# Hybrid decoder layer on one core: score blocks of gated linear attention collected in a compact tile

## The chip, the cores and the metric

The kernel runs on one core of one Trainium2 chip. The metric is device time in microseconds (us) of one execution. A core has five engines with instruction streams of their own: TensorE (PE in the profile; its weight loads are listed as PEld), VectorE (DVE), ScalarE (ACT), GpSimd (POOL) and SyncE (SP), which here issues the DMAs. They wait for each other through semaphores.

## The reference

One decoder layer over 2048 frames with 16 meta tokens in front, all float32. A norm and one combined projection feed three mixers: attention with forget gates (FoX, 8 heads), gated linear attention (GLA, 4 heads, 64 keys, 128 values each) and a gated linear recurrence (LRU, width 1024). Their gated outputs go through one output projection, a norm and the residual sum.

```
proj = rms_norm(h, pre_g) @ w_in
fq, fk, fv, ff, fg, gq, gk, gv, ga, gg, lx, lg = split(proj)
y_fox = fox_attention(fq, fk, fv, log_sigmoid(ff + b_f)) * silu(fg)
log_a = log_sigmoid(ga @ w_a2 + b_a) / 16
o     = gla(gq, gk, gv, log_a)        # S_t = diag(a_t) S_(t-1) + k_t^T v_t;  o_t = q_t S_t
y_gla = o * rsqrt(mean(o*o) + eps) * gla_norm_g * silu(gg)
y_lru = rg_lru(conv(lx), w_r, b_r, w_i, b_i, lam) * silu(lg)
out   = h + rms_norm(concat(y_fox, y_gla, y_lru) @ w_out, post_g)
```

The change is in the GLA part. Inside 128 positions the kernel computes a masked score block: element (s, t), for s <= t, is the sum over the 64 keys of k_s q_t exp(b_t - b_s), with b the running sum of log_a.

## The kernel before

**Stages.** Projections (`proj_cm`, L465; `proj_tm`, L477) are 24 matmuls each: 8 slices of the model width, and fp16 high and low halves in three products. The mixers run one after the other: GLA first (100 to 545 us in the profile), then LRU, FoX, and the output projection. The program is a list of jobs (`jobs`, L194 to 217). A job has weight loads, a `prep` generator that issues the projections for it, a `mix` generator with the mixer's own arithmetic, and two numbers. `merge` (L155) steps the mix of one job and the prep of the next in turn: over the first `n_main` steps of the mix it spreads `n_fill` steps of the prep, and what is left of either is issued at the end. A step is what stands between two `yield`s; a projection is one to three of them. GLA has eight such mixes: two pairs of heads (hp 0 and 1), each over four chunks of 512 positions; with them stand the projections of the next chunk, beside the last one those of the first LRU job. LRU has 40 jobs (8 width tiles, 5 pieces each). Within an engine instructions run in the order of issue, which a scheduler has settled when the program is built.

**A GLA chunk (`gla_mix`).** The two heads of a pair hold 64 partitions each, and a chunk is four blocks i of 128 positions. A block's 128x128 scores are built by levels. The two widest (64 and 32) are plain rectangles off the diagonal. The diagonal 32x32 blocks take level 0 (the plain product, of which only the diagonal counts) and five levels 16, 8, 4, 2, 1, each right for another part of the block. For a level, GpSimd subtracts (L956, L957), ScalarE takes the exponential (L958) and VectorE multiplies with keys and queries (L959, L960) into a tile `lv`; TensorE then computes sixteen 32x32 blocks a head, 32 matmuls (`L992`, 64x32 weights and 32 columns, float32) into PSUM, with one bank for each head (tag `st`, two banks). VectorE copies each into `at`, a [128, 4, 128] tile of SBUF for each head, where a mask of bytes says so: `copy_predicated` L999, four partition groups of 32 by two heads, so 8 instructions a level of 32 partitions x 4 x 32 elements. The next level's scores take the same two banks, so they wait for those copies. For level 0 VectorE multiplies by the identity instead (L1009, 8 instructions), TensorE also computes the wide rectangles (L1005), and ScalarE copies these into `at` (L1014). GpSimd has set `at` to zero before (L978).

At the chunk's end 16 matmuls with `at` (L1023) and 16 with the carried state S (L1027), float32, add up to the chunk's output in two banks (`pv`). This closing run is issued without a `yield` in it. What follows (L1033 to L1048) squares, gates and norms it.

**Other names.** `gate` is the output gate (tanh on ScalarE L501, product on VectorE L502), `gv` the evacuated value projection (ScalarE L754), `mx` banks for small sums. `norm_apply` (L389 to L393) normalizes the next 512 columns of the input and splits them in fp16 halves; it runs inside the prep of the first chunks. `fa_mix` (L645) multiplies the 16-row gate projection by w_a2 (L659), in a bank of tag `st`, which ScalarE evacuates (L660); its log-sigmoid ends in L679. PSUM has eight banks: `pj` (projections), `mx`, `st` and `pv`, two each.

Of the kernel before, what the change touches and what calls it, by code (L numbers as in the profile page):

```python
# [40 lines left out]
LEVELS = (64, 32, 16, 8, 4, 2, 1)  # L41
# [38 lines left out]
GAP = 2  # L80
# [7 lines left out]
class Ctx:  # L88
# [6 lines left out]


BUFS = {"A0": 3, "A2": 3, "KA": 6, "KB": 6, "QA": 2, "QB": 2, "B0": 2, "B1": 2, "B2": 2, "B3": 2, "V": 6, "G": 2, "R": 1,
        "T": 3, "ZZ": 4, "WC": 1, "OO": 3, "OX": 2, "LV": 5, "AT": 4, "GV": 6, "GG": 6, "GS": 6, "M": 1, "MV": 1, "YG": 2, "RS": 2, "ZS": 1, "ZA": 2, "PT": 6, "ED": 2, "KT": 1, "Z": 1, "WH": 1, "WL": 1, "XC": 4, "X": 16, "L0": 4, "L1": 4, "L2": 2, "L3": 2, "L4": 6}


def unit(k, tag, shape, dt=F32, name=None):
    wide = tag in ("QA", "QB", "KA", "KB", "WC", "OO", "OX", "T", "Z", "ZZ", "WH", "WL")
# [64 lines left out]
def hybrid_kernel(tc, xT, x, w_grp, w_fa, vecs, w_a2, w_r, w_i, w_out, post_g, masks, out, yD=None):  # L167
    nc = tc.nc
    with ExitStack() as es:
        k = Ctx()  # L170
# [20 lines left out]
        norm_scale(k)  # L191
        start = beside(first_project(k), gla_first(k, FIRST_FA, 0), FA0)

        jobs = [([], start, chain(gla_meta(k, 0), gla_mix(k, 0, 0)), 11 + GAP, 0)]  # L194
        for c in range(1, NCH):
            f = [(NM + CH * c + CH // 2 * i, CH // 2) for i in range(2)]
            load = {2: [("gk", 1), ("gv", 1, 0), ("gv", 1, 1), ("gq", 1), ("gg", 1, 0), ("gg", 1, 1)]}
            jobs.append((load.get(c, []), chain(fa_project(k, f), beside(gla_project(k, 0, c), gla_first(k, f, c), FA1)),
                         gla_mix(k, 0, c), 8 + GAP, 28))
        sums = forget_sums(k)  # L200
        for c in range(NCH):
            load = {2: [("lx", 0), ("lg", 0)]}
# [737 lines left out]
def gla_mix(k, hp, c):  # L940
# [35 lines left out]
    for h in range(2):  # L976
        with k.tc.issue_after(pool):
            nc.gpsimd.memset(at[h], 0.0)  # L978
    steps = (0,) + LEVELS[2:]
    for li, C in enumerate(steps):  # L980
# [14 lines left out]
        for h in range(2):
            hs = slice(64 * h, 64 * h + 64)
            if C:
                for s in parts:
                    nc.vector.copy_predicated(at[h][s, :, s], k.masks[s, li - 1:li, s].to_broadcast([32, 4, 32]),  # L999
                                              sps[h][s, :, s])  # L1000
                continue
            for W, xw in wide:
                for i in range(4):
                    for s0 in range(0, P, 2 * W):
                        nc.tensor.matmul(out=sps[h][s0:s0 + W, i, s0 + W:s0 + 2 * W],  # L1005
                                         lhsT=xw[hs, i * P + s0:i * P + s0 + W],
                                         rhs=xw[hs, i * P + s0 + W:i * P + s0 + 2 * W], start=True, stop=True)
            for s in parts:
                nc.vector.tensor_tensor(at[h][s, :, s], sps[h][s, :, s],  # L1009
                                        k.ident[s, s].unsqueeze(1).to_broadcast([32, 4, 32]), op=ALU.mult)  # L1010
# [623 lines left out]
```

## Time and profile before

| | us |
|---|---|
| timed runs | 2058.44, 2058.95, 2049.12 (median 2058.44) |
| the profiled execution's own time | 2055.92 |
| its span, first to last recorded instruction | 2054.2 |
| TensorE busy | 1930.0 (94%) |
| VectorE busy | 1324.5 (64%) |
| ScalarE busy | 995.9 (48%) |
| GpSimd busy | 584.0 (28%) |
| GLA stage | 100 to 545 |

The profile records one execution. Busy time of an engine is the sum of its instructions; a matmul's end is modelled. "Idle before" is the time an engine stood still in front of a group of instructions, with the engine and the line that ended it. The granted clock is the share of TensorE's full clock (2.4 GHz) that it was given in a stretch; 0.50 is 1.2 GHz.

### The profile page before, as it was taken

To read this page: it belongs to the slowest core of one execution; us is meant where nothing else is said; L and a number is where in the kernel's file an instruction comes from. 1 tells how busy PE (TensorE), PEld (TensorE's weight loads), DVE (VectorE), ACT (ScalarE), POOL (GpSimd) and SP (SyncE) were. 2 spreads that over 40 slices of the span, in tenths; PEclk is the share of its full clock that TensorE was granted. 3 is DMA by queue.
4 is the path that set the end of the run, shared out by engine and by line. 5 is a ranking of instruction groups with operands and counts; after the bars stand their busy time and mean duration, and the time that the engine had idled before them with its cause. 6 is when DMAs were issued, how large, how long until landed. Compare 5 with 4: busy or idle time off the path is not lost. (4 is left out here: it accounts for less than half of the span.)

```text
span 2054.2 us, 39995 instructions
## 1 busy us (share of the span) xinstructions
PE 1930.0 (94%) x16240; PEld 1024.9 (50%) x16240; DVE 1324.5 (64%) x3038; ACT 995.9 (48%) x1489; POOL 584.0 (28%) x571
## 2 busy tenths in 40 slices
PE   7888989999999999999999999999999968989998
PEld 5555666556555556556434443444344323634443
DVE  6777464666687778784576357435734565887664
ACT  7744632335588888872334233422332356544441
POOL 3334122223333333331112111211121113443532
PEclk9899889899899999999999999999999989999999
DMA  6200120111211111110022002100200132734321
GB/s 221 68 9 28 40 83 29 34 51 33 90 46 42 42 42 46 42 63 7 13 56 67 13 12 56 49 13 22 73 2 22 32 112 74 251 114 131 122 91 62
DMA packets 92266, 123.37 MB, mean 60 GB/s; under 512 B 16936, under 2 KB 59624, under 8 KB 92080
## 3 DMA queue, kind: packets, MB, share of 16 engines
q1 hardware_dynamic: 92080, 120.81, 18.7%
q8 instruction: 127, 2.08, 0.4%
q14 instruction: 59, 0.48, 0.1%
HBM read 94.03 MB, written 26.65 MB: 59 GB/s over the span
## 5 line engine op out<-in xcount | busy, mean ns | idle before, releaser
L465 PE MATMUL pj<-xhl,whl 128*128 128x512 f16 (+3 forms) x3960 | 807.0, 356 | 19.4 <-DVE at L999 7.1
L465 PEld LDWEIGHTS <-whl 128*128 128x128 f16 x3984 | 365.8, 98 | 394.5 <-issue 59.9
L1243 ACT ACTIVATE pt<-sq,consts 128x1024 f32<-128x1024 f32 (+4 forms) x176 | 163.0, 926 | 281.2 <-PE sq L1241 152.3
L1185 DVE CUSTOM_DVE_ANT_0 mj<-mq,CB 128x512 bf16<-128x512 f32 (+4 forms) x344 | 189.7, 580 | 85.5 <-PE mq L1181 47.0
L1251 POOL TENSOR_TENSOR za<-za,pt 128x512 f32<-128x512 f32 (+1 forms) x80 | 98.2, 1227 | 397.4 <-ACT pt L1243 361.7
L477 PEld LDWEIGHTS <-xhl 128*128 128x128 f16 (+1 forms) x3264 | 191.1, 99 | 39.4 <-issue 34.6
L1251 DVE TENSOR_TENSOR za<-za,pt 128x512 f32<-128x512 f32 (+3 forms) x208 | 124.9, 627 | 118.0 <-ACT pt L1243 117.8
L477 PE MATMUL pj<-whl,xhl 128*128 128x128 f16 (+1 forms) x3024 | 196.0, 223 | 3.3 <-ACT gv L754 3.3
L1259 PE MATMUL fv<-pt,fv 128*64 128x512 f32 (+4 forms) x704 | 170.3, 531 | 0.4 <-ACT pt L1243 0.4
L1564 PEld LDWEIGHTS <-whl 128*128 128x128 f16 x1008 | 98.8, 98 | 126.3 <-issue 10.3
L1235 PE MATMUL sq<-QA,KA 64*128 64x512 f16 (+4 forms) x1032 | 128.5, 342 | 13.5 <-ACT pt L1243 13.1
L1564 PE MATMUL pj<-ts,whl 128*128 128x512 f16 x576 | 129.8, 385 | 6.0 <-ACT ts L1337 4.6
L999 DVE COPY_PREDICATED at<-consts,st 32x128 f32<-32x128 uint8 x320 | 94.6, 296 | 19.6 <-PE st L992 10.7
L543 DVE SCALAR_TENSOR_TENSOR xc<-lx,consts,xc 128x448 f32<-128x448 f32 (+1 forms) x120 | 94.8, 790 | 3.5
L1564 PE MATMUL pj<-xhl,whl 128*128 128x512 f16 x432 | 95.4, 379 | 0.0
L1544 PE MATMUL pj<-xhl,yhl 128*128 128x256 f16 (+1 forms) x576 | 89.2, 312 | 0.3 <-DVE xhl L1338 0.3
L1278 POOL TENSOR_TENSOR fo<-fo,rz 128x512 f32<-128x512 f32 x16 | 21.3, 1334 | 221.3 <-DMA rz<-rowD 165.9
L1235 PEld LDWEIGHTS <-KA 64*128 64x128 f16 (+1 forms) x1032 | 42.1, 94 | 79.8 <-issue 59.9
L1526 POOL TENSOR_TENSOR o<-o,xt 128x512 f32<-128x512 f32 x31 | 50.8, 1657 | 99.3 <-DVE o L1523 48.9
L958 ACT ACTIVATE lv<-lv 128x512 f32<-128x512 f32 x56 | 34.9, 626 | 91.0 <-POOL lv L957 90.9
L501 ACT ACTIVATE gate<-pj,consts 128x512 f32<-128x512 f32 (+2 forms) x72 | 46.1, 640 | 67.6 <-PE pj L465 67.1
L1235 PE MATMUL sq<-QA,KX 64*128 64x512 bf16 (+4 forms) x344 | 68.3, 341 | 8.8 <-DMA QA<-dr 8.8
(260 smaller groups left out, 2920.4 us busy)
## 6 DMA issues: line engine op xcount, KB each, us to landing
raw<-in_w_grp_dram SPq DMA_DIRECT2D x44, 512.0 KB
raw<-in_w_out_dram SPq DMA_DIRECT2D x32, 512.0 KB
y<-yD SPq DMA_DIRECT2D x32, 512.0 KB
CB<-c32D SPq DMA_DIRECT2D x32, 256.0 KB
xt<-in_x_dram SPq DMA_DIRECT2D x16, 512.0 KB
out_dram<-o SPq DMA_DIRECT2D x32, 256.0 KB
yD<-yl SPq DMA_DIRECT2D x32, 224.0 KB
xr<-in_xT_dram SPq DMA_DIRECT2D x24, 256.0 KB
```

Of the source, the lines that this page charges most:

```text
L465: nc.tensor.matmul(out=ps, lhsT=a[:, kt, 0:m], rhs=b[:, kt, u0:u0 + n], start=i == 0, stop=i == 23)
L477: nc.tensor.matmul(out=ps, lhsT=a[:, kt, u0:u0 + m], rhs=b[:, kt, :], start=i == 0, stop=i == 23)
L543: nc.vector.scalar_tensor_tensor(out=xc, in0=lx[:, j:j + n], scalar=cw(j), in1=xc, op0=ALU.mult, op1=ALU.add)
L999: nc.vector.copy_predicated(at[h][s, :, s], k.masks[s, li - 1:li, s].to_broadcast([32, 4, 32]), sps[h][s, :, s])
L1185: nc.vector.tensor_tensor_reduce(out=junk[:, h, 0:n], in0=ps[:, h, 0:n], in1=d.cb[pc][:, h, 0:n], scale=1.0, scalar=-3e38, op0=ALU.add, op ...
L1235: nc.tensor.matmul(out=sp[0:m, h, off:], lhsT=a[j // 4][hs, kk], rhs=b[hs, off:], start=i == 0, stop=i == 3 and d < 0)
L1243: nc.scalar.activation(pt[0:m, :, off:], sp[0:m, :, off:], AF.Exp, scale=K.esc[0:m])
L1251: eng.tensor_tensor(out=za[h][0:m, off:], in0=za[h][0:m, off:], in1=pt[0:m, h, off:], op=ALU.add)
L1259: nc.tensor.matmul(out=pv[hs, off1:], lhsT=V1[0:m1, j1 % 4, hs], rhs=pt1[0:m1, h, off1:], start=j1 == 0, stop=j1 == nj - 1)
L1526: eng.tensor_tensor(out=o, in0=o, in1=xt[:, h, :], op=ALU.add)
L1544: nc.tensor.matmul(out=po, lhsT=a, rhs=cut(w, r), start=i == 0, stop=i == 3 * OT - 1)
L1564: nc.tensor.matmul(out=ps, lhsT=a[:, kt, :], rhs=b(kt), start=kt + j == 0, stop=(kt, j) == (KT - 1, 2))
```

## The change

**Score blocks.** The two tiles `at` become one [128, 8, 128]. The diagonal blocks are gathered in a new compact tile `ac` [128, 8, 32]: partition group s of 32 rows holds its own 32 columns. Masks and identity are laid out in the same way at the start of the program (`load_consts`). All 32x32 blocks of a level go to the same 128 columns of a bank, so that one `copy_predicated` for each head takes all 128 partitions: 2 instead of 8 a level. PSUM: the two `st` banks become one pair `gs`. Level 0 has a pair for itself, and the five levels share a second allocation of it, four levels side by side in slots of 128 columns (the fifth takes the first slot again). At the chunk's end eight copies, four on VectorE and four on ScalarE, bring `ac` into `at`, and a `yield` follows. The closing run gets a `yield` after two of its four blocks.

**Steps.** n_main goes from 8 + GAP to 10 + GAP (11 to 13 in the first chunk of a pair of heads), n_fill from 28, 34 and 24 to 23, 25 and 20, the number of steps that the prep has. The first two LRU jobs become one job, whose prep stands beside the last GLA mix. LRU jobs without a store take n_main 3 in place of 4.

**Bank of the gate projection.** `fa_mix` takes its bank from `pj` in place of `st`.

```
-BUFS: "AT": 4                      +BUFS: "AT": 2 (wide), "AC": 2
 def hybrid_kernel
-   ... gla_mix(k, 0, c), 8 + GAP, 28))
+   ... gla_mix(k, 0, c), 10 + GAP, 23))
-   ... gla_mix(k, 1, c), 8 + GAP, 24))
+   ... gla_mix(k, 1, c), 10 + GAP, 20))
-   jobs.append((load.get((t, c), []), lru_project(k, t, c), lru_mix(k, t, c, ...), 4, 6))
+   if (t, c) == (0, 1):
+       w, prep0, mix0, n0, n_fill = jobs.pop()
+       jobs.append((w, chain(prep0, prep), chain(mix0, mix), n0 + 4, n_fill + 6))
+   else:
+       jobs.append((load.get((t, c), []), prep, mix, 4 if flush else 3, 6))
 def load_consts
-   nc.gpsimd.tensor_copy(k.masks, mf[:, 2:, :])
+   for s0 in range(0, P, 32):
+       s = slice(s0, s0 + 32)
+       nc.gpsimd.tensor_copy(k.masks[s], mf[s, 2:, s])
+       nc.vector.tensor_copy(k.identc[s], k.ident[s, s])
 def fa_mix
-   pz = bank(k, "st")
+   pz = bank(k)
 def gla_mix
-   at = [unit(k, "AT", [P, 4, P], name="at") for _ in range(2)]
+   at = unit(k, "AT", [P, 8, P], name="at").rearrange("p (h i) t -> p h i t", h=2)
+   ac = unit(k, "AC", [P, 8, 32], name="ac").rearrange("p (h i) t -> p h i t", h=2)
    for li, C in enumerate(steps):
-       sps = [blocks(bank(k, "st")) for _ in range(2)]
+       if li < 2:
+           sp = pair(k, "gs")
+           if C: sv = sp.rearrange("p h (l i t) -> p l h i t", l=4, t=32)
+           else: sb = sp.rearrange("p h (i t) -> p h i t", t=P)
+       sc = sv[:, (li - 1) % 4] if C else sb[:, :, :, 0:32]
-       matmul(out=sps[h][s, i, s], lhsT=xk[hs, e], rhs=xq[hs, e])
+       matmul(out=sc[s, h, i], lhsT=xk[hs, e], rhs=xq[hs, e])
-       for s in parts: copy_predicated(at[h][s, :, s], k.masks[s, li - 1:li, s], sps[h][s, :, s])
+       copy_predicated(ac[:, h], k.masks[:, li - 1:li, :], sc[:, h])
-       for s in parts: tensor_tensor(at[h][s, :, s], sps[h][s, :, s], k.ident[s, s], op=mult)
+       tensor_tensor(ac[:, h], sc[:, h], k.identc, op=mult)
        yield
+   for j, s in enumerate(parts):
+       for h in range(2):
+           (nc.vector.tensor_copy if j < 2 else nc.scalar.copy)(out=at[s, h, :, s], in_=ac[s, h])
+   yield
    for i in range(4):
        matmul(os[h][:, s], lhsT=V[h][:, i, :], rhs=at..., start=True, stop=False)
        matmul(os[h][:, s], lhsT=S[hs, i, :], rhs=qd[hs, s], start=False, stop=True)
+       if i == 1: yield
```

Lines move by 11 in the helpers and by up to 22 in `gla_mix`: L465 becomes L476, L477 L488, L660 L671, L999 L1012, L1009 L1024, L1014 L1029, L1023 L1043, L1027 L1047; the copies out of `ac` are L1034.

The order of instructions on an engine, before and after, at three places. First VectorE at the end of the fifth chunk (first chunk of the second pair of heads), before; L959 and L960 are level products, L502 a gate, L1035 the chunk's output:

```order
L999 COPY_PREDICATED at<-consts,st 32x4x32 x8
L959 TENSOR_TENSOR lv<-lv,ks 128x16x16
L960 TENSOR_TENSOR lv<-lv,qs 128x16x16
L999 COPY_PREDICATED at<-consts,st 32x4x32 x8
L959 TENSOR_TENSOR lv<-lv,ks 128x32x8
L960 TENSOR_TENSOR lv<-lv,qs 128x32x8
L502 SCALAR_TENSOR_TENSOR gate<-gate,pj 128x512
L999 COPY_PREDICATED at<-consts,st 32x4x32 x8
L959 TENSOR_TENSOR lv<-lv,ks 128x64x4
L960 TENSOR_TENSOR lv<-lv,qs 128x64x4
```

and after, where L970 and L971 are the level products, L1012 the masked copies and L513 the gate:

```order
L1012 COPY_PREDICATED ac<-consts,gs 128x128 x2
L971 TENSOR_TENSOR lv<-lv,qs 128x8x32
L971 TENSOR_TENSOR lv<-lv,qs 128x16x16
L970 TENSOR_TENSOR lv<-lv,ks 128x32x8
L971 TENSOR_TENSOR lv<-lv,qs 128x32x8
L1012 COPY_PREDICATED ac<-consts,gs 128x128 x2
L1034 COPY at<-ac 32x4x32 x4
L970 TENSOR_TENSOR lv<-lv,ks 128x64x4
L971 TENSOR_TENSOR lv<-lv,qs 128x64x4
L513 SCALAR_TENSOR_TENSOR gate<-gate,pj 128x512
L1057 SCALAR_TENSOR_TENSOR yg<-pv,consts,gate 128x512 x2
```

The gate, which stood between the level products and the last copies, now comes behind the copies out of `ac`.

Second TensorE at the same place, before: the last projection, and the start of the closing run (the run goes on as it begins, with 16 of each line):

```order
L465 LDWEIGHTS whl
L465 MATMUL pj<-xhl,whl 128x512
L1023 MATMUL pv<-at,gv 128x128
L1027 MATMUL pv<-qd,S 128x128
L1023 MATMUL pv<-at,gv 128x128
L1027 MATMUL pv<-qd,S 128x128
L1023 MATMUL pv<-at,gv 128x128 x2
L1027 MATMUL pv<-qd,S 128x128
L1023 MATMUL pv<-at,gv 128x128
L1027 MATMUL pv<-qd,S 128x128
L1023 MATMUL pv<-at,gv 128x128
L1027 MATMUL pv<-qd,S 128x128 x2
```

and after:

```order
L476 LDWEIGHTS whl
L476 MATMUL pj<-xhl,whl 128x512
L1043 MATMUL pv<-at,gv 128x128 x2
L1047 MATMUL pv<-qd,S 128x128 x2
L1043 MATMUL pv<-at,gv 128x128 x2
L1047 MATMUL pv<-qd,S 128x128 x2
L476 LDWEIGHTS whl
L476 MATMUL pj<-xhl,whl 128x512
L476 LDWEIGHTS whl
L476 MATMUL pj<-xhl,whl 128x512
```

The run is cut behind the second block; 8 projections follow, and then the other half. In front of the first half stand 24 projections where 8 stood before.

Third VectorE in the second chunk, where the norm of the next input columns is applied (L389, L393; after L400, L404), before:

```order
L389 SCALAR_TENSOR_TENSOR xr<-xr,consts,mx 128x512
L393 TENSOR_TENSOR xhl<-xr,xhl 128x512
L389 SCALAR_TENSOR_TENSOR xr<-xr,consts,mx 128x512 x3
L393 TENSOR_TENSOR xhl<-xr,xhl 128x512
L389 SCALAR_TENSOR_TENSOR xr<-xr,consts,mx 128x512
L393 TENSOR_TENSOR xhl<-xr,xhl 128x512
L1009 TENSOR_TENSOR at<-st,consts 32x4x32 x8
L959 TENSOR_TENSOR lv<-lv,ks 128x128x2
L960 TENSOR_TENSOR lv<-lv,qs 128x128x2
L959 TENSOR_TENSOR lv<-lv,ks 128x256
L960 TENSOR_TENSOR lv<-lv,qs 128x256
L999 COPY_PREDICATED at<-consts,st 32x4x32 x13
```

and after:

```order
L400 SCALAR_TENSOR_TENSOR xr<-xr,consts,mx 128x512 x3
L404 TENSOR_TENSOR xhl<-xr,xhl 128x512
L400 SCALAR_TENSOR_TENSOR xr<-xr,consts,mx 128x512
L404 TENSOR_TENSOR xhl<-xr,xhl 128x512
L400 SCALAR_TENSOR_TENSOR xr<-xr,consts,mx 128x512 x3
L404 TENSOR_TENSOR xhl<-xr,xhl 128x512
L400 SCALAR_TENSOR_TENSOR xr<-xr,consts,mx 128x512
L690 SCALAR_TENSOR_TENSOR z<-z,e 128x1024
L404 TENSOR_TENSOR xhl<-xr,xhl 128x512
L1012 COPY_PREDICATED ac<-consts,gs 128x128 x2
L852 SCALAR_TENSOR_TENSOR b<-consts,z 128x128 x4
L970 TENSOR_TENSOR lv<-lv,ks 128x256
```

The norm stood ahead of level 0 (L1009) before and stands now between the masked copies of two levels (rows ahead of it: L1012 x2). L690, the last step of the log-sigmoid (L679 before), stands inside it.

## Rows read from the trace of the kernel before

**Rows 1.** The page: span, and TensorE's busy time with the other engines'.
```profile
span 2054.2 us, 39995 instructions
PE 1930.0 (94%) x16240; PEld 1024.9 (50%) x16240; DVE 1324.5 (64%) x3038; ACT 995.9 (48%) x1489; POOL 584.0 (28%) x571
```

**Rows 2.** Stretches: us, busy us of engines (instructions), clock, DMA share, GB/s.
```profile
100.00:545.00 445.00, 408.84 (x6157) 265.14 (x6157) 278.21 (x759) 175.99 (x298) 125.42 (x164) 0.90 0.13 39
545.00:1290.00 745.00, 731.36 (x4832) 380.33 (x4830) 511.52 (x1155) 436.27 (x599) 206.40 (x235) 1.00 0.14 44
```

**Rows 3.** Groups, 100 to 545 us: busy us, mean ns | idle before, who ended it.
```profile
L465 PE MATMUL pj<-xhl,whl 128*128 128x512 f16 x648 | 157.1, 395 | 9.1 <-DVE at L999 7.1 <-ACT at L1014 2.0
L999 DVE COPY_PREDICATED at<-consts,st 32x128 f32<-32x128 uint8 x320 | 94.6, 296 | 19.6 <-PE st L992 10.7
...
L1023 PE MATMUL pv<-at,gv 128*128 128x128 f32 x128 | 34.9, 387 | 8.3 <-DVE at L999 8.2
...
L992 PE MATMUL st<-lv 64*32 64x32 f32 x2560 | 33.2, 204 | 9.8 <-DVE at L999 8.9 <-DVE lv L960 0.9
...
L960 DVE TENSOR_TENSOR lv<-lv,qs 128x256 f32<-128x256 f32 x51 | 30.5, 605 | 0.2
...
L959 DVE TENSOR_TENSOR lv<-lv,ks 128x256 f32<-128x256 f32 x51 | 26.1, 512 | 16.5 <-ACT lv L958 15.5
...
L1009 DVE TENSOR_TENSOR at<-st,consts 32x128 f32<-32x128 f32 x64 | 18.3, 287 | 12.8 <-PE st L1005 11.2
...
L389 DVE SCALAR_TENSOR_TENSOR xr<-xr,consts,mx 128x512 f32<-128x512 f32 x16 | 11.2, 738 | 3.2 <-PE mx L380 3.2
...
L393 DVE TENSOR_TENSOR xhl<-xr,xhl 128x512 f16<-128x512 f32 x8 | 7.6, 947 | 3.4 <-ACT xhl L391 3.4
...
L659 PE MATMUL st<-ga,wa 16*128 16x256 f32 x16 | 6.6, 578 | 2.2 <-ACT at L1014 1.3 <-PE pj L477 0.9
...
L477 PE MATMUL pj<-whl,xhl 128*16 128x128 f16 x48 | 5.5, 295 | 3.3 <-ACT gv L754 3.3
...
L679 DVE SCALAR_TENSOR_TENSOR z<-z,e 128x1024 f32<-128x1024 f32 x3 | 4.6, 1535 | 0.2 <-ACT e L678 0.2
...
L465 PE MATMUL pj<-xhl,whl 128*128 128x16 f16 x24 | 0.8, 171 | 1.9 <-DVE gate L502 1.9
```

**Rows 4.** Timeline, fifth chunk's end: start, us, instruction, count [idle before, releaser].
```profile
381.47 0.76 PE L992 MATMUL st<-lv 64*32 64x32 f32 x64
...
382.16 1.90 PE L465 MATMUL pj<-xhl,whl 128*128 128x512 f16 x8
...
382.31 0.42 DVE L959 TENSOR_TENSOR lv<-lv,ks 128x256 f32<-128x256 f32 x1
...
382.66 0.83 DVE L960 TENSOR_TENSOR lv<-lv,qs 128x256 f32<-128x256 f32 x1
...
383.52 0.69 DVE L502 SCALAR_TENSOR_TENSOR gate<-gate,pj 128x512 f32<-128x512 f32 x1
...
384.12 2.58 DVE L999 COPY_PREDICATED at<-consts,st 32x128 f32<-32x128 uint8 x8
...
385.54 0.46 PE L1023 MATMUL pv<-at,gv 128*128 128x128 f32 x2 [1.48 <-DVE at L999]
```

**Rows 5.** Stretches, as rows 2: five of the eight closing runs.
```profile
205.60:214.80 9.20, 9.20 (x34) 6.61 (x36) 1.91 (x6) 0.00 (x0) 0.00 (x0) 0.53 0.00 0
274.40:283.90 9.50, 9.50 (x33) 6.80 (x34) 2.14 (x10) 0.00 (x0) 0.00 (x0) 0.50 0.23 82
332.20:337.70 5.50, 5.46 (x33) 4.04 (x34) 1.87 (x6) 0.00 (x0) 0.00 (x0) 1.00 0.00 0
385.50:393.90 8.40, 8.36 (x32) 6.04 (x32) 1.87 (x6) 0.00 (x0) 0.00 (x0) 0.59 0.00 0
523.80:533.30 9.50, 9.50 (x32) 6.83 (x32) 5.12 (x10) 1.05 (x1) 0.00 (x0) 0.50 0.03 9
```

**Rows 6.** Timeline, as rows 4: a run of short projections.
```profile
306.89 2.85 PE L477 MATMUL pj<-whl,xhl 128*128 128x128 f16 x48
```

More of the change, by code (lines that the diff above doesn't have):

```diff
@@ L97 @@
 BUFS = {"A0": 3, "A2": 3, "KA": 6, "KB": 6, "QA": 2, "QB": 2, "B0": 2, "B1": 2, "B2": 2, "B3": 2, "V": 6, "G": 2, "R": 1,
-        "T": 3, "ZZ": 4, "WC": 1, "OO": 3, "OX": 2, "LV": 5, "AT": 4, "GV": 6, "GG": 6, "GS": 6, "M": 1, "MV": 1, "YG": 2, "RS": 2, "ZS": 1, "ZA": 2, "PT": 6, "ED": 2, "KT": 1, "Z": 1, "WH": 1, "WL": 1, "XC": 4, "X": 16, "L0": 4, "L1": 4, "L2": 2, "L3": 2, "L4": 6}
+        "T": 3, "ZZ": 4, "WC": 1, "OO": 3, "OX": 2, "LV": 5, "AT": 2, "AC": 2, "GV": 6, "GG": 6, "GS": 6, "M": 1, "MV": 1, "YG": 2, "RS": 2, "ZS": 1, "ZA": 2, "PT": 6, "ED": 2, "KT": 1, "Z": 1, "WH": 1, "WL": 1, "XC": 4, "X": 16, "L0": 4, "L1": 4, "L2": 2, "L3": 2, "L4": 6}
 def unit(k, tag, shape, dt=F32, name=None):
-    wide = tag in ("QA", "QB", "KA", "KB", "WC", "OO", "OX", "T", "Z", "ZZ", "WH", "WL")
+    wide = tag in ("AT", "QA", "QB", "KA", "KB", "WC", "OO", "OX", "T", "Z", "ZZ", "WH", "WL")
     n = 1
@@ L192, in hybrid_kernel @@
         start = beside(first_project(k), gla_first(k, FIRST_FA, 0), FA0)
-        jobs = [([], start, chain(gla_meta(k, 0), gla_mix(k, 0, 0)), 11 + GAP, 0)]
+        jobs = [([], start, chain(gla_meta(k, 0), gla_mix(k, 0, 0)), 13 + GAP, 0)]
         for c in range(1, NCH):
@@ L204, in hybrid_kernel @@
                 jobs.append(([], chain(gla_project(k, 1, -1), gla_project(k, 1, 0)),
-                             chain(gla_meta(k, 1), gla_mix(k, 1, 0)), 11 + GAP, 34))
+                             chain(gla_meta(k, 1), gla_mix(k, 1, 0)), 13 + GAP, 25))
             else:
-                jobs.append((load.get(c, []), gla_project(k, 1, c), gla_mix(k, 1, c), 8 + GAP, 24))
+                jobs.append((load.get(c, []), gla_project(k, 1, c), gla_mix(k, 1, c), 10 + GAP, 20))
         lru0 = len(jobs)
@@ L215, in hybrid_kernel @@
                     load = {(7, 0): [("fk", 0), ("fv", 0)], (7, 2): [("fq", 0), ("fg", 0)]}
-                jobs.append((load.get((t, c), []), lru_project(k, t, c),
-                             lru_mix(k, t, c, (5 * t + c) % 2 == 1), 4, 6))
+                flush = (5 * t + c) % 2 == 1
+                prep, mix = lru_project(k, t, c), lru_mix(k, t, c, flush)
+                if (t, c) == (0, 1):
[3 more added lines that the diff above has]
+                    jobs.append((load.get((t, c), []), prep, mix, 4 if flush else 3, 6))
         for p in range(4):
@@ L291, in load_consts @@
     nc = k.nc
-    k.masks = carve(k, (len(LEVELS) - 2) * P // 4).bitcast(U8).rearrange("p (l t) -> p l t", t=P)
+    k.masks = carve(k, (len(LEVELS) - 2) * 8).bitcast(U8).rearrange("p (l t) -> p l t", t=32)
+    k.identc = carve(k, 32)
     mf = unit(k, "T", [P, len(LEVELS), P], name="mf")
     nc.sync.dma_start(out=mf, in_=k.ins["masks"])
-    nc.gpsimd.tensor_copy(k.masks, mf[:, 2:, :])
+    for s0 in range(0, P, 32):
+        s = slice(s0, s0 + 32)
+        nc.gpsimd.tensor_copy(k.masks[s], mf[s, 2:, s])
+        nc.vector.tensor_copy(k.identc[s], k.ident[s, s])
 def pow2_scale(k, sq, scale, inv, mul=None):
@@ L973, in gla_mix @@
     k.st["S"] = nS
-    at = [unit(k, "AT", [P, 4, P], name="at") for _ in range(2)]
-    for h in range(2):
-        with k.tc.issue_after(pool):
-            nc.gpsimd.memset(at[h], 0.0)
+    at = unit(k, "AT", [P, 8, P], name="at").rearrange("p (h i) t -> p h i t", h=2)
+    ac = unit(k, "AC", [P, 8, 32], name="ac").rearrange("p (h i) t -> p h i t", h=2)
+    with k.tc.issue_after(pool):
+        nc.gpsimd.memset(at, 0.0)
     steps = (0,) + LEVELS[2:]
+    parts = [slice(s0, s0 + 32) for s0 in range(0, P, 32)]
     for li, C in enumerate(steps):
@@ L983, in gla_mix @@
             x = level(steps[li + 1])
-        sps = [blocks(bank(k, "st")) for _ in range(2)]
-        parts = [slice(s0, s0 + 32) for s0 in range(0, P, 32)]
+        if li < 2:
+            sp = pair(k, "gs")
+            if C:
+                sv = sp.rearrange("p h (l i t) -> p l h i t", l=4, t=32)
+            else:
+                sb = sp.rearrange("p h (i t) -> p h i t", t=P)
+        sc = sv[:, (li - 1) % 4] if C else sb[:, :, :, 0:32]
         for i in range(4):
@@ L991, in gla_mix @@
                     e = slice(i * P + s.start, i * P + s.stop)
-                    nc.tensor.matmul(out=sps[h][s, i, s], lhsT=xk[hs, e], rhs=xq[hs, e], start=True, stop=True)
-        if not C:
-            yield
[L995 to L1010, printed above, removed]
+                    nc.tensor.matmul(out=sc[s, h, i], lhsT=xk[hs, e], rhs=xq[hs, e], start=True, stop=True)
@@ new lines, in gla_mix @@
+        if C:
+            for h in range(2):
+                nc.vector.copy_predicated(ac[:, h], k.masks[:, li - 1:li, :].to_broadcast([P, 4, 32]), sc[:, h])
+        else:
+            yield
+            for h in range(2):
+                hs = slice(64 * h, 64 * h + 64)
+                for W, xw in wide:
+                    for i in range(4):
+                        for s0 in range(0, P, 2 * W):
+                            nc.tensor.matmul(out=sb[s0:s0 + W, h, i, s0 + W:s0 + 2 * W],
+                                             lhsT=xw[hs, i * P + s0:i * P + s0 + W],
+                                             rhs=xw[hs, i * P + s0 + W:i * P + s0 + 2 * W], start=True, stop=True)
+            for h in range(2):
+                nc.vector.tensor_tensor(ac[:, h], sc[:, h], k.identc.unsqueeze(1).to_broadcast([P, 4, 32]),
+                                        op=ALU.mult)
@@ L1011, in gla_mix @@
             for W, _ in wide:
                 for s0 in range(0, P, 2 * W):
-                    blk = slice(s0, s0 + W), slice(0, 4), slice(s0 + W, s0 + 2 * W)
-                    nc.scalar.copy(out=at[h][blk], in_=sps[h][blk])
+                    for h in range(2):
+                        nc.scalar.copy(out=at[s0:s0 + W, h, :, s0 + W:s0 + 2 * W],
+                                       in_=sb[s0:s0 + W, h, :, s0 + W:s0 + 2 * W])
         yield
+    for j, s in enumerate(parts):
+        for h in range(2):
+            (nc.vector.tensor_copy if j < 2 else nc.scalar.copy)(out=at[s, h, :, s], in_=ac[s, h])
@@ L1022, in gla_mix @@
         for h in range(2):
-            nc.tensor.matmul(out=os[h][:, s], lhsT=V[h][:, i, :], rhs=at[h][:, i, :], start=True, stop=False)
+            nc.tensor.matmul(out=os[h][:, s], lhsT=V[h][:, i, :], rhs=at[:, h, i, :], start=True, stop=False)
         for h in range(2):
@@ L1027, in gla_mix @@
             nc.tensor.matmul(out=os[h][:, s], lhsT=S[hs, i, :], rhs=qd[hs, s], start=False, stop=True)
+        if i == 1:
+            yield
     sqs = []
```

2 lines of the change are left out of this document (1 added, 1 removed).

## The prediction

> **What bounds the kernel now.** I read the 40 slices first, then busy time by stretches, then the groups by line with what ended their idle time, then the timeline of one chunk end. TensorE is busy 94% of the span [rows 1], so time can only come from its idle gaps and from stretches at the lower of its two clock levels. The stretch from 100 to 545 us holds all eight chunk mixes that the edits touch: in its 445 us TensorE is busy 408.84, so 36.2 idle, at a mean granted clock of 0.90. The LRU stage behind it, 745 us, is 731.36 busy at 1.00 [rows 2]; there is little to win there, whatever order its jobs have.
>
> Who ends the idle time in that stretch: VectorE's L999, the masked copies of the 32x32 score blocks. It ends 8.2 us in front of L1023 (the products with V at a chunk's end), 8.9 in front of the scores L992 and 7.1 in front of projections L465 [rows 3]. The fifth chunk's end shows how: after the last scores TensorE has 8 projections (1.90 us), while VectorE has two level products and a gate (0.42, 0.83, 0.69) and then 8 masked copies (2.58); L1023 starts after 1.48 us of idle [rows 4]. Eight copies and two level products are 8 x 0.296 + 0.512 + 0.605 = 3.49 us a level, against 0.76 + 1.90 = 2.66 us that TensorE has there. VectorE sets the pace.
>
> The gap is not the whole price. The run of L1023 and L1027 that closes a chunk takes 5.5 us at granted clock 1.00 (2.4 GHz; the row at 332.2 stands for four such runs), but 9.2, 9.5, 8.4 and 9.5 us where the clock falls to the 1.2 GHz level for most or all of it [rows 5]. Three of those four runs stood right behind a wait for L999, the fourth behind a 3.3 us wait for a 16-row value projection (L477, ended by ScalarE's gv) [rows 3].
>
> **The change, part by part.**
>
> *Score blocks side by side.* The masked copy now takes all 128 partitions at once: 80 copies in place of 320, each with the same 128 elements per partition. A row for that shape does not exist; from the row for 32 partitions I take the same 0.296 us [rows 3]. Lower end: no cheaper than that row. Upper end: the nearest wide row, a level product with 256 elements at 0.605; 80 x 0.605 is still 48 us below 320 x 0.296. The diagonal products go from 64 to 16 at 0.287. New are 64 copies out of the compact tile at the chunk's end, 32 on VectorE (taken as 0.287, the row of L1009; ends 0 and 0.605) and 32 on ScalarE, at the same 0.287 some 9 us on an engine busy 176 of 445 us [rows 2, 3]. VectorE is relieved of 240 x 0.296 + 48 x 0.287 - 32 x 0.287 = 75.6 us of 278. The memset becomes 8 of twice the width in place of 16, on GpSimd, which is busy 125 of the 445 us [rows 2] and works a level ahead: 0.
>
> *Chunk end.* Behind the last scores VectorE now has 2 copies and 4 compact copies, 0.59 + 1.15 = 1.74 us, or 3.68 with the three operations of rows 4 ahead of them. In the new order 24 projections stand there in the fifth chunk (24 x 1.90/8 = 5.7 us) and in no chunk fewer than 13 (3.1). So the 8.2 us in front of L1023 go: **-8.2**. The run itself is cut by projections after two of four blocks. If the runs start without a gap, I take them to be of the full-clock kind: (9.2 + 9.5 + 8.4 + 9.5) - 4 x 5.5 = **-14.6**. Bounds: 0, if the clock falls by the small float32 products alone, and -14.6. I stand near the upper end, because the full-clock ones of before are those that follow no gap or a short one.
>
> *Levels.* Each level still waits for the copies of the level before, and the pair of banks now holds both heads, so a turn is scores, two copies, scores. With little else in VectorE's queue that is 0.59 us; the new order puts four projections or more (0.95 us) between. Hence most of the 8.9 + 7.1 goes. Not in the first two chunks: there the norm of the next input chunk stands in VectorE's queue ahead of a level's copies: 8 x 0.738 + 4 x 0.947 + 1.535 = 11.2 us [rows 3], while TensorE has about 8.5 us of work there (some 130 short projections at 2.85/48 and one set of scores [rows 6]). I leave 3.5 us in each of the two and 2 for the rest: 16 - 9 = **-7**; bounds 0 and -16.
>
> *Clock beside the levels.* 0.10 of 445 us is 44.5 us of lost clock; the four low-clock closings account for 0.47 x 9.2 + 0.50 x 9.5 + 0.41 x 8.4 + 0.50 x 9.5 = 17.3 of it. Of the other 27 the part that trails those closings and the stalls in chunks five and six goes; I take a quarter, **-7**; bounds 0 and -27.
>
> *Gate projections' small bank.* The w_a2 products (L659) leave the score banks and share those of the projections: 3.3 us of waits on the block copies (1.3 at L659, 2.0 at L465) turn into waits on ScalarE's own evacuations, with projections between in the new order. 0; bounds -3.3 and +6 (twelve late products at 0.5).
>
> *Even spread, two LRU jobs beside the last chunk.* No instruction is added. The 5.2 us of waits at the 16-row projections (1.9 and 3.3) lie at a job's border that now has work to both sides; half: **-2.6**, bounds 0 and -5.2. The two jobs beside the last chunk take their share of the levels' term above. SP's queue gets the same loads in the same order, one job earlier; no DMA ends an idle gap of TensorE in rows 3. The eight small copies of the masks and the diagonal at the start: **+1**.
>
> Sum: -8.2 - 14.6 - 7 - 7 - 2.6 + 1 = -38.4. The profiled execution took 2055.9 us, 0.1% below the median of the three timed runs (2058.4), so the two may be taken for one another: 2055.9 - 38.4 = 2017.5, **2018 us**.
>
> **Rivals.**
>
> *Slower: the packed bank.* A level's four projections no longer cover the turn, because with both heads in one pair the scores of one head can no longer be computed while the other is copied. If VectorE has the two level products and an evacuation of 0.7 us between, its turn is 0.59 + 1.12 + 0.70 = 2.4 us against 0.95 of cover: 1.5 us idle at 40 levels, +60, less the 16 and 8.2 that go: 2092 us. It decides from 24.2/40 = 0.6 us of idle per level on. For it: in the first two chunks the queue is that full. Against it: from the third chunk on the cover is mostly 24 or 48 short projections, and the level products are done ahead. The Trainium skill says the same in "PSUM — Partial Sum Buffer", section "PSUM bank collisions raise a hardware error": guard by bank and quadrant, not by address, since an access to other columns of the same bank still collides; so four levels beside each other in one bank buy no overlap. By that rule the copies of rows 4 would stand between any two levels after the change as before; the trace agrees as far as it goes (scores start after the copies of two levels earlier, from the same banks), and what it costs is the 0.6 us above.
>
> *No more than the chunk end.* The clock falls in any case, since the float32 products are the last thing before each fall, and the halves of the run are at the lower clock as the wholes were. Then -8.2 - 7 + 1: 2042 us. For it: the mean of the whole stretch is 0.90 [rows 2], which is more loss than these closings account for. Against it: the four closings at full clock.
>
> *More.* With VectorE out of the way three quarters of the idle time and of the lost clock go: 27 + 0.75 x 44.5 x 0.86 (the closing of 9.2 us lost 4.3 by the clock and 3.7 in time) = 56: 2000 us. The floor, all of both, is 1982.
>
> **How the numbers follow.** Forecast 0.55 (2018, own range 2006 to 2032), more 0.17, no more than the chunk end 0.22 (2030 to 2060), slower 0.06. The range leaves out about 2 in 10: 1994 to 2050. What a measurement can tell from no change is 0.5%, 10.3 us. Faster by more: 0.55 + 0.17 + half of the 0.22 = 0.83; within: 0.10; slower: 0.07.
>
> **What would show it.** L1043 (the former L1023) with next to no idle in front; most runs of it at clock 1.00; masked copies 80 at about 0.3 us; remaining idle in the first two chunks, ended by L1012; mean clock of the stretch 0.94 or more. It is wrong if L1012 ends more than 20 us of idle, if the halves of the closing run stay at 0.5, or if waits on ScalarE's L671 (the former L660) appear in three chunks with more than 2 us each.

## The result and the profile after

The changed kernel takes 2023.93 us (median of four runs, 2022.69 to 2028.36) against 2055.28 us: ratio 0.9854, 95% interval 0.9822 to 0.9886, or 30 us less (23 to 37). The forecast was 2018 us. From one profiled execution to the other it is 33.3 us: the span falls from 2054.2 [rows 1] to 2020.9 us. First the page of the changed kernel, then (in windows, PE busy and number, granted clock, DMA share, GB/s) the GLA stage from 78 us to its last closing run and the LRU stage behind it, of the kernel before and of the changed one.

```profile
span 2020.9 us, 39720 instructions
PE 1898.0 (94%) x16240; PEld 1010.4 (50%) x16240; DVE 1248.9 (62%) x2786; ACT 1004.8 (50%) x1521; POOL 591.0 (29%) x566
```

```profile
78.00:533.40 455.40, 418.29 (x6287) 0.90 0.14 42
533.40:924.10 390.70, 387.57 (x2166) 1.00 0.15 50
```

```profile
78.00:496.60 418.60, 388.43 (x6302) 0.95 0.14 46
496.60:886.20 389.60, 384.65 (x2149) 1.00 0.15 50
```

The GLA stage gives 36.8 us: 29.9 of TensorE's busy time at about as many matmuls (6287 and 6302 records), and only 6.9 of its idle time (37.1 to 30.2). LRU does not change. What lies behind 886.2 takes 4.6 us longer than what lay behind 924.1 before (1134.7 and 1130.1 us); in the traces of the twelve kernels below this tail has 1128 to 1136 us, so the difference is not put down to the change. (The prediction called 545 to 1290 us the LRU stage; LRU ends at 924, FoX follows. No term used it.)

The groups of the stage in the changed kernel (busy us, mean ns | idle before, who ended it), which answer to [rows 3]:

```profile
L476 PE MATMUL pj<-xhl,whl 128*128 128x512 f16 x675 | 159.1, 386 | 0.0
...
L1009 PE MATMUL gs<-lv 64*32 64x32 f32 x2560 | 32.0, 204 | 22.7 <-DVE ac L1012 16.5 <-ACT at L1029 3.1 <-DVE consts L314 2.2
...
L1043 PE MATMUL pv<-at,gv 128*128 128x128 f32 x128 | 21.3, 289 | 0.0
L1012 DVE COPY_PREDICATED ac<-consts,gs 128x128 f32<-128x128 uint8 x80 | 19.6, 292 | 18.4 <-PE gs L1009 18.4
...
L1047 PE MATMUL pv<-qd,S 64*128 64x128 f32 x128 | 15.7, 323 | 0.0
...
L1034 DVE COPY at<-ac 32x128 f32<-32x128 f32 x32 | 10.4, 361 | 0.1
...
L670 PE MATMUL pj<-ga,wa 16*128 16x256 f32 x24 | 9.9, 496 | 4.3 <-DVE ks L741 2.4 <-ACT z L671 1.9
...
L476 PE MATMUL pj<-xhl,whl 128*128 128x16 f16 x24 | 0.9, 169 | 0.0
```

A masked copy over 128 partitions takes 0.292 us, as one over 32 did (0.296), so that the 80 take 19.6 us where the 320 took 94.6. L1043 has no idle time in front of it. The waits on masked copies between levels are all still there: 8.9 in front of the scores and 7.1 in front of projections before, 16.5 in front of the scores now.

The closing runs are where most of the busy time went. One of the sixteen halves (the others read 2.09 to 2.18 us at 1.00 as well; all sixteen are 33.6 us, where the eight runs of before were 58.8):

```profile
309.75:311.84 2.09, 2.09 (x18) 1.00 0.00 0
```

That is 4.2 us for a closing run where [rows 5] have 5.5 at full clock. The timeline shows why: TensorE alternates between L1023 with 128 rows and L1027 with 64, before mostly by twos (first fence, from the run at 332.2), now by fours (second fence).

```profile
332.24 0.46 PE L1023 MATMUL pv<-at,gv 128*128 128x128 f32 x2 [1.05 <-DVE at L999]
332.63 0.48 PE L1027 MATMUL pv<-qd,S 64*128 64x128 f32 x2
333.04 0.49 PE L1023 MATMUL pv<-at,gv 128*128 128x128 f32 x2
```

```profile
309.75 0.61 PE L1043 MATMUL pv<-at,gv 128*128 128x128 f32 x4
310.29 0.49 PE L1047 MATMUL pv<-qd,S 64*128 64x128 f32 x4
310.71 0.71 PE L1043 MATMUL pv<-at,gv 128*128 128x128 f32 x4
```

From one start to the next, a group of two L1027 takes 0.41 us (332.63 to 333.04) and a group of four L1047 0.42. Before there are 12 groups in such a run, now 8. One run of `gla_old` (below) is in 10 groups, at full clock, with its next instruction at 261.21:

```profile
256.35:261.21 4.86, 4.86 (x33) 1.00 0.54 169
```

From its start to the next instruction a run takes 5.43 us in 12 groups (332.24), 4.86 in 10, and 4.23 in 8 (`gla_old` at 306.32): some 0.3 us a group. The Trainium skill has a rule in "TensorEngine Tiling (Array Packing)", section "Key Properties": a change of tiling mode drains TensorE. The rows fit it, if the two row counts are two modes; it states no price, and no run here changes the order alone.

### The profile page after: what moved, and what is told of

Same layout as the page of the kernel before. It is cut to its first block, busy times and chain, and to the rows that moved or that the text cites. A ratio compares the mean times of both kernels' runs of the same rounds, so it can differ in the third digit from the quotient of the medians.

```text
span 2020.9 us, 39720 instructions
## 1 busy us (share of the span) xinstructions
PE 1898.0 (94%) x16240; PEld 1010.4 (50%) x16240; DVE 1248.9 (62%) x2786; ACT 1004.8 (50%) x1521; POOL 591.0 (29%) x566
## 5 line engine op out<-in xcount | busy, mean ns | idle before, releaser
L476 PE MATMUL pj<-xhl,whl 128*128 128x512 f16 (+3 forms) x3960 | 800.1, 354 | 10.0 <-ACT whl L433 6.5
L476 PEld LDWEIGHTS <-whl 128*128 128x128 f16 x3984 | 364.4, 98 | 381.5 <-issue 52.8
L1207 DVE CUSTOM_DVE_ANT_0 mj<-mq,CB 128x512 bf16<-128x512 f32 (+4 forms) x344 | 189.7, 579 | 86.2 <-PE mq L1203 48.3
L488 PEld LDWEIGHTS <-xhl 128*128 128x128 f16 (+1 forms) x3264 | 192.7, 100 | 35.3 <-issue 30.7
L488 PE MATMUL pj<-whl,xhl 128*128 128x128 f16 (+1 forms) x3024 | 198.3, 224 | 0.0
L1566 PEld LDWEIGHTS <-yhl 128*128 128x128 f16 x576 | 56.0, 100 | 41.9 <-issue 13.1
L589 POOL TENSOR_TENSOR v<-a 128x448 f32<-128x448 f32 (+1 forms) x40 | 38.6, 965 | 128.2 <-ACT a L587 128.2
```

The costliest lines, as they stand in the source:

```text
L476: nc.tensor.matmul(out=ps, lhsT=a[:, kt, 0:m], rhs=b[:, kt, u0:u0 + n], start=i == 0, stop=i == 23)
L488: nc.tensor.matmul(out=ps, lhsT=a[:, kt, u0:u0 + m], rhs=b[:, kt, :], start=i == 0, stop=i == 23)
L1207: nc.vector.tensor_tensor_reduce(out=junk[:, h, 0:n], in0=ps[:, h, 0:n], in1=d.cb[pc][:, h, 0:n], scale=1.0, scalar=-3e38, op0=ALU.add, op ...
L1566: nc.tensor.matmul(out=po, lhsT=a, rhs=cut(w, r), start=i == 0, stop=i == 3 * OT - 1)
```

## The experiments

Ratios are to the kernel before, with 95% intervals; 0.9854 is the changed kernel's. Each edit is to the changed kernel unless it says otherwise.

**The break taken out.**

```
-        if i == 1:
-            yield
```

> The changed kernel, but the closing run of a chunk (L1043, L1047) is issued in one piece, without the break after two blocks; what stands in front of it stays. If the low clock of the closing runs came from the waits in front of them, nothing comes back: next to no idle time in front of L1043, closing runs of about 4.9 us at granted clock 1.00, 2024 us, 5 either way. Rival, that a float32 run of full length pulls the clock down by itself and the break is what saved it: four to eight of the runs at about 0.5 and 9 us, 4 us more each, 2040 to 2058 us.

2037.57 us, 0.9911 (0.9890 to 0.9932), 12 us more than the changed kernel. The time lies between the two forecasts. Seven of the eight closing runs stay at 1.00 and take 4.2 us, so the break does not guard the clock. The one in the last chunk, behind a wait of 2.87 us, falls to 0.50. The other loss is in front of the first level behind a level 0 (L1009 behind ScalarE's copies L1029: 3.1 with the break, 10.0 here):

```profile
L1009 PE MATMUL gs<-lv 64*32 64x32 f32 x2560 | 31.4, 205 | 27.2 <-DVE ac L1012 15.5 <-ACT at L1029 10.0 <-DVE consts L314 1.7
...
L1043 PE MATMUL pv<-at,gv 128*128 128x128 f32 x128 | 24.2, 314 | 2.9 <-DVE at L1034 2.9
```

**A forced wait in front of the closing run.**

```
+    for _ in range(5):
+        for s in parts[:2]:
+            for h in range(2): nc.vector.tensor_copy(out=at[s, h, :, s], in_=ac[s, h])
```

> The changed kernel, but at a chunk's end VectorE makes its four copies out of the compact tile five times more in front of the real ones (20 copies of about 0.36 us, 7.2 us a chunk; same values), so that the closing run comes too late for the projections in front of it. If a wait in front of the closing run is what costs the clock: 15 to 30 us of idle time in front of L1043 over the eight chunks, and the first halves behind it at 0.5 to 0.6 in place of 1.00, 2 to 4 us more each: 2055 to 2085 us. Rival, that the clock has another cause: the idle time alone, halves of the closing run at 2.5 us and 1.00, 2040 to 2053 us.

2058.14 us, 1.0021 (1.0008 to 1.0034): the whole gain is gone. The closing products stand behind 17.8 us of waits. The first three rows below are first halves behind a wait of 5.15 us (at 270.67), of none (325.93) and of 2.73 us (381.68); the fourth is the second half behind the third:

```profile
L1047 PE MATMUL pv<-at,gv 128*128 128x128 f32 x128 | 26.5, 340 | 17.8 <-DVE at L1038 17.8
```

```profile
270.67:274.48 3.81, 3.81 (x17) 0.50 0.41 138
325.93:328.02 2.09, 2.09 (x18) 1.00 0.00 0
381.68:385.03 3.35, 3.35 (x17) 0.57 0.00 0
388.35:390.76 2.41, 2.41 (x18) 0.86 0.00 0
```

Same matmuls, same order; the clock is low behind a long wait. In this kernel the first halves behind waits of 2.49 us read 0.68 and 0.72, the run of the last chunk, in one piece behind 2.68, 0.50, and the first halves behind 1.60, 0.70 and none 1.00. The second halves have no wait and read 1.00, but for the 0.86 above. In the GLA stage idle time grows by 19 us (to 49.3) and busy time by 21 (to 409.6): a wait costs about twice its length here. The theory held, though not every first half fell; its rival did not hold.

**VectorE's relief undone.**

```
-            nc.vector.copy_predicated(ac[:, h], ..., sc[:, h])
+            for s in parts: nc.vector.copy_predicated(ac[s, h], ..., sc[s, h])
```

and the diagonal products (L1024) likewise.

> The changed kernel with its steps, banks and compact tile, but the masked copies and diagonal products are made as before, one for each group of 32 partitions: 240 more masked copies and 48 more products of about 0.29 us, 84 us on VectorE. If VectorE's relief is what lets TensorE run on: a level's turn takes 2.4 us of copies in place of 0.6, waits in front of the scores L1009 go from 22.7 us to 40 or more, some runs fall to the lower clock, 2050 us or more. Rival, that the even steps and the projections in front of the closing run do it: 2024 to 2032 us.

2053.72 us, 0.9995 (0.9984 to 1.0005). Even steps, break, bank pair and compact tile without the wide copies are together worth nothing. The theory held, with 33.7 us of waits where 40 was forecast and 5.4 in front of the closing runs. In the GLA stage idle time grows by 18 us (to 48.3) and busy time by 19 (to 407.4).

```profile
L1013 DVE COPY_PREDICATED ac<-consts,gs 32x128 f32<-32x128 uint8 x320 | 94.9, 296 | 16.4 <-PE gs L1009 7.4
...
L1009 PE MATMUL gs<-lv 64*32 64x32 f32 x2560 | 31.5, 203 | 33.7 <-DVE ac L1013 27.8 <-ACT at L1031 5.8
```

**All step numbers of before.**

```
-   13 + GAP, 0 | 10 + GAP, 23 | 13 + GAP, 25 | 10 + GAP, 20 ; first two LRU jobs joined ; LRU 3
+   11 + GAP, 0 |  8 + GAP, 28 | 11 + GAP, 34 |  8 + GAP, 24 ; apart ; LRU 4
```

> The changed kernel with the numbers of before: steps of main and fill 8 + GAP with 28, 34 and 24, the first two LRU jobs apart, LRU jobs with 4. Compact tile, bank, break and closing copies stay. The projections then run out sooner, about 9 (2.1 us) are left in front of a closing run. If the spread is a part of the gain: 3 to 8 us of idle time in front of L1043, three or four closing runs at the lower clock (4 us each), 2038 to 2050 us. Rival, that the cheaper copies do it alone: up to 2030 us.

2009.34 us, 0.9781 (0.9762 to 0.9800): 15 us less than the changed kernel. The theory (2038 to 2050) fell; the rival's "up to 2030" takes the time in, but neither forecast a gain. These numbers, taken together, cost time. The next two kernels divide it.

**Only the GLA numbers of before**, with the joined LRU job and LRU's 3 kept.

> The changed kernel with only the step numbers of the GLA jobs from before (8 + GAP main steps; 28, 34, 24 fill steps); the joined LRU job beside the last GLA mix and LRU's 3 stay. If the even spread of the projections is what cost the 15 us by which the run with all numbers of before was faster: about 2009 us, waits in front of the scores near 16 us in place of 22.7. Rival, that the joined LRU job or LRU's 3 cost them: 2020 to 2028 us.

2011.15 us, 0.9790 (0.9767 to 0.9813): the GLA numbers alone are 13 us. Waits on the masked copies fall from 16.5 to 3.5 us:

```profile
L1009 PE MATMUL gs<-lv 64*32 64x32 f32 x2560 | 30.5, 201 | 14.5 <-ACT at L1029 10.5 <-DVE ac L1012 3.5 <-issue 0.6
```

In the first chunk, 6, 4, 5 and 4 projections stand between its levels with the even spread, 13, 16, 16 and 8 with the numbers of before; in front of the closing run 9 are left in three chunks and 16 or more in the others, and none at the break, which is enough beside VectorE's 2.0 us of copies there (2 x 0.292 + 4 x 0.361): waits are 2.0 us in all, all eight closing runs at 1.00.

**Only the LRU jobs of before**, the first two apart and all with 4.

> The changed kernel with its even spread, but the first two LRU jobs apart again and LRU jobs with 4 main steps. If the even spread cost the 15 us: 2024 us, 4 either way. Rival, that the joined LRU job or LRU's 3 cost them: 2006 to 2013 us.

2021.14 us, 0.9834 (0.9812 to 0.9855): not to be told from the changed kernel. No gain or cost of the joined job is shown.

**Banks by turns.** The scores of levels 16, 4 and 1 go to the two banks `pv`, free till the closing run, those of 8 and 2 to the pair `gs`.

```
+        if li == 1: pv4 = [bank(k, "pv").rearrange("p (l i t) -> p l i t", l=4, t=32) for _ in range(2)]
-        sc = sv[:, (li - 1) % 4] if C else sb[:, :, :, 0:32]
+        sc = level 0: sb[:, h, :, 0:32];  li odd: pv4[h][:, li // 2];  li even: gs[:, li // 2 - 1, h]
```

> The changed kernel, but the scores of the levels 16, 4 and 1 go to the two banks of the closing run (pv, free till then) and those of 8 and 2 to the pair gs, so that no level waits for the masked copies of the level before. If the packed pair makes the waits: those in front of the scores fall from 22.7 us to 8 or less, and with them some of the low clock: 2003 to 2013 us. Rival, that VectorE's queue makes them (the norm ahead of the copies), and a wait only comes a level later: 15 us of waits or more, 2018 to 2027 us.

2002.04 us, 0.9741 (0.9717 to 0.9765): 23 us less than the changed kernel, with the same steps. The waits in front of the scores fall from 22.7 to 7.6, the stage's mean clock is 0.97:

```profile
L1016 PE MATMUL pv<-lv 64*32 64x32 f32 x1536 | 18.7, 199 | 1.9 <-DVE ac L1019 1.9
L1016 PE MATMUL gs<-lv 64*32 64x32 f32 x1024 | 12.6, 202 | 5.7 <-DVE ac L1019 4.4 <-ACT at L1036 0.9 <-issue 0.2
```

```profile
78.00:477.90 399.90, 382.87 (x6306) 0.97 0.15 48
```

So the one pair for all levels makes most of the waits between them. The rule of the Trainium skill in "PSUM — Partial Sum Buffer", section "PSUM bank collisions raise a hardware error", is to guard by bank and quadrant, not by address. The changed kernel keeps it (scores into other columns of a bank wait for its copies), and 23 us is what that costs here; no run breaks it.

**Only the numbers, on the kernel before** (fill 23, 25 and 20, first two LRU jobs joined, LRU's 3).

> The kernel before with only the numbers of the change: fill steps 23, 25 and 20, the first two LRU jobs joined, LRU's 3. Narrow copies straight into the wide tile, two banks for two heads, no break, as before. 16 to 24 projections then stand in front of a closing run in place of 7 to 25. If the spread helps where VectorE is behind: the 8 us of waits in front of L1023 go and two or three of the low-clock closing runs with them, 2032 to 2046 us. Rival, that holding projections back costs as much between the levels as it gives at the end: 2050 us or more.

2040.27 us, 0.9933 (0.9911 to 0.9954). The time is as forecast, its mechanism not: waits at the closing products do not go but grow (8.3 to 11.0, below; 4.8 of them inside the runs). What falls are the waits in front of 128x512 projections (9.1 to 5.0) and the closing runs themselves, from 58.8 us to 47.2 with the waits inside, most of the 12.3 us between the two profiled executions. Two of eight are at the lower clock in place of four, and seven of eight alternate by fours. So the order by fours comes with these numbers alone as well as, in `old_spread`, without them; what makes the scheduler choose it stays open.

```profile
L998 PE MATMUL st<-lv 64*32 64x32 f32 x2560 | 33.8, 200 | 14.9 <-DVE at L1005 6.9 <-DVE lv L966 3.8 <-ACT at L1020 2.5
...
L1029 PE MATMUL pv<-at,gv 128*128 128x128 f32 x128 | 27.3, 333 | 11.0 <-DVE at L1005 11.0
```

One of the runs stays at 1.00 behind a wait of 2.01 us:

```profile
261.31:266.61 5.30, 4.46 (x32) 1.00 0.00 0
```

**Banks by turns with all step numbers of before.**

> The two that were faster together: level scores in banks by turns (pv and gs), and the step numbers of before, LRU jobs apart. If the two cut different waits, the gains over the changed kernel (22 and 15 us) add up in part: 1988 to 1997 us. Rival, that the numbers of before only helped because more projections stood between levels that waited for each other, which the banks by turns have already cured: 1999 to 2008 us.

2002.11 us, 0.9755 (0.9737 to 0.9773), as the rival said: not to be told from banks by turns with the even spread (0.9741). Once the levels take turns, no effect of the numbers on the time is left to see.

**Banks by turns, the norm in four parts.**

```
-   if (hp, h, i) == (0, 0, 1): norm_root; norm_apply(k, c + 2)
+   at steps (0,0,1), (0,0,2), (0,0,3), (0,1,0): norm_apply(k, c + 2, two of the eight slices)
```

> Level scores in banks by turns with the even spread, and the norm of the next input columns issued in four parts of two slices over four projection steps in place of one block of 11 us on VectorE. If that block makes the waits that are left in the first two chunks (2.2, 1.9, 2.3 and 2.1 us) and the low clock behind them: 1990 to 1997 us. Rival, that they have another cause: 1999 to 2005 us.

2004.53 us, 0.9774 (0.9755 to 0.9792), as the rival said: waits of 2 to 3 us remain in the first two chunks, behind other instructions.

**All three.**

> All three: banks by turns, norm in four parts, step numbers of before. If each cuts waits of its own: 1984 to 1992 us. Rival, that the even spread is as good once no wait is left: within 3 us of the run with the even spread, the banks by turns and the norm in four parts.

1999.43 us, 0.9747 (0.9726 to 0.9768). Not to be told from banks by turns alone (0.9741), so the three do not add up.

**The gate projections' bank taken back** (`pz = bank(k, "st")`).

> The changed kernel with the bank of the gate projections taken back to the tag st (L670). By the prediction the move of the bank is worth nothing: 2024 us, 4 either way. Rival, that the two pj banks make the 4.3 us of waits in front of L670 and the lower clock behind them (95 to 110 and 228 to 235 us): 2012 to 2019 us.

2029.24 us, 0.9888 (0.9869 to 0.9907): the rival fell, and the time is 1 us above the theory's range. If anything the change's bank is the better one by 7 us, but the intervals overlap.

## Why the prediction was right, and where its steps were not

The time lies in the likeliest case's own range, and the mechanism of its largest terms, at the chunk's end, was right. That the sum came so near is in part luck: 10.4 us of a shorter run that I had not seen stand against 7.5 us of levels and 6.0 of other waits that I had wrong. Term by term, from the two profiled executions:

| term | forecast | measured |
|---|---|---|
| waits in front of the closing run | -8.2 | -8.3 (to 0.0) |
| closing runs | -14.6 | -25.2: -14.8 clock, -10.4 order |
| waits of levels | -7 | +0.5 (16.0 to 16.5) |
| busy time beside | -7 | -4.7 (29.9 less 25.2) |
| gate projections' bank | 0 | 0 (4.2 to 4.3, with what stood at L465) |
| 16-row projections | -2.6 | -5.2 |
| other waits in the stage (L1029 3.1, L314 2.2, rest) | 0 | +6.0 (idle -6.9 less the rows above) |
| start; LRU and behind | +1 | +3.5 |
| whole span | -38.4 | -33.3 |

**Chunk end and closing runs: right, and shown.** All sixteen halves are at 1.00. The forced wait shows that a wait in front of a half brings its clock down; undoing the wide copies shows that without VectorE's relief the rest of the change gains nothing (29 us of 30 go). The rival "no more than the chunk end", in which the float32 products pull the clock down by themselves, falls with the sixteen halves, all behind projections and all at 1.00, and with the seven uncut runs at 1.00 without the break. How long a wait does it is not sharp: 1.48, 1.77 and 1.72 us sufficed in front of uncut runs of before (at 385.5, 205.6 and 523.8 us) [rows 4, 5], 1.60 did not in front of a half, nor 2.01 in front of a run of `spread_only`. So the wait is not all that decides; what else does stays open. What I did not see is that at full clock the run itself gets 1.3 us shorter, eight times 5.5 - 4.2 = 10.4, with the new order by fours. I took the cut at two of four blocks to be what matters in the run; the run in one piece stays at 1.00 too, and alternates by fours as well.

**Levels: the step that failed.** I set a turn at 0.59 us, "with little else in VectorE's queue", covered by four projections (0.95). VectorE's queue in the first chunk of the changed kernel, while TensorE waits from 120.21 to 126.80 us for the L1012 in it:

```profile
118.45 2.17 DVE L690 SCALAR_TENSOR_TENSOR z<-z,e 128x1024 f32<-128x1024 f32 x1
120.55 0.47 DVE L1024 TENSOR_TENSOR ac<-gs,consts 128x128 f32<-128x128 f32 x2
120.95 1.35 DVE L852 TENSOR_TENSOR_SCAN b<-consts,z 128x128 f32<-128x128 f32 x4
122.23 0.39 DVE L970 TENSOR_TENSOR lv<-lv,ks 128x256 f32<-128x256 f32 x1
122.54 1.26 DVE L971 TENSOR_TENSOR lv<-lv,qs 128x256 f32<-128x256 f32 x1
123.72 0.83 DVE L970 TENSOR_TENSOR lv<-lv,ks 128x256 f32<-128x256 f32 x1
124.48 0.84 DVE L971 TENSOR_TENSOR lv<-lv,qs 128x256 f32<-128x256 f32 x1
125.24 1.09 DVE L868 TENSOR_TENSOR ed<-ks,ed 128x512 f32<-128x512 f32 x1
126.26 0.48 DVE L1012 COPY_PREDICATED ac<-consts,gs 128x128 f32<-128x128 uint8 x2
```

```profile
126.80 0.89 PE L1009 MATMUL gs<-lv 64*32 64x32 f32 x64 [6.59 <-DVE ac L1012]
```

Not the norm, which I named, is ahead of the copies while TensorE waits (it ended at 118.5), but the next chunk's sums (L852), its level products and its decays (L868): a step's VectorE work of both generators. Whether these would have been done sooner without the norm in front of them, this kernel does not show; splitting the norm, tried with banks by turns, gives nothing. The first two chunks keep 12.8 us of the 16.5, where I left 7. (In the part on the score blocks one bound is misadded: 80 x 0.605 is 46 us below 320 x 0.296, not 48. Nothing rests on it.)

**The packed bank: its mechanism was there, its size was not.** I gave it 0.06 because 0.6 us at each of 40 levels would be needed to lose. In the kernel before, the scores of a level start ahead of the copies of the level before in 7 of 32 cases, as here in the fifth chunk (scores of the second level, copies of the first):

```profile
366.14 0.46 PE L992 MATMUL st<-lv 64*32 64x32 f32 x32
...
367.50 2.58 DVE L999 COPY_PREDICATED at<-consts,st 32x128 f32<-32x128 uint8 x8
```

(So the sentence ahead of the prediction, that the next level's scores wait for those copies, holds for a part of the levels only.) In the changed kernel no scores start before those copies have ended, in any of the 32 cases; with banks by turns 11 start ahead of them again. The pair costs 23 us against banks by turns, some 0.6 us a level: the gain could have been 53 us in place of 30. What the two heads in one pair cost by themselves no run shows.

**Even spread: wrong sign.** I counted half of 5.2 us for it. Those 5.2 went, but the spread was not needed for it: with the GLA numbers of before (`gla_old`) the waits at the 16-row projections are 0.3 us, and with the new numbers on the kernel before (`spread_only`) they are 0.0. And the spread takes projections from between the first chunk's levels. It costs 13 us in this kernel, brings 14 in the one before, where most of it lies in the closing runs, and nothing that can be seen once the levels take turns.

## What to carry to other kernels

Where a small stage alternates TensorE and another engine through one PSUM bank, making the other engine four times cheaper removes only the waits that were due to its rate; the ones due to its queue stay until other work of the first engine covers them (as with the old step numbers) or the two engines work in different banks, which cost no bank here because those of a later step stood free. In front of such products waits of up to 5.2 us cost about double their length here: look behind them for the lower clock. A table of step numbers is worth what the waits around it make of it: time it again after each change of what waits.

## What was not expected of the hardware

A masked copy costs the same over 128 partitions as over 32 (0.292 and 0.296 us at 128 elements in a partition), and so does the product with the identity (0.283 and 0.287), while a plain copy over 32 partitions from SBUF to SBUF takes 0.361 us on VectorE. Two or four matmuls of 64 rows between 128-row ones take the same 0.42 us. With the forced wait, TensorE's first closing products read 1.00 behind waits up to 1.6 us, 0.68 to 0.72 behind 2.49, and 0.50 to 0.57 behind 2.7 to 5.2 us; in other kernels of this document uncut runs read 0.59 behind 1.48 us and 1.00 behind 2.01.
